# Moving the gate projections of a hybrid encoder layer beside its SSM, and two small transfers to another queue

## The chip, the cores and the metric

The kernel runs on one core of a Trainium2 chip. The metric is the time on the device of one execution, in microseconds (us), as the median of several runs. The engines are PE (TensorE), DVE (VectorE), ACT (ScalarE), POOL (GpSimd) and SP (SyncE, which here issues nearly all transfers).

## What is computed

One encoder layer in float32 on a sequence of 512 tokens of width 1024:

```python
h = h + 0.5 * swiglu_1(rms_norm(h))
u = rms_norm(h)
q, k, v, x_ssm, g_attn, g_ssm = split(u @ W_in)
y_attn = block_gqa(rope(qk_norm(q)), rope(qk_norm(k)), v) @ W_attn_branch
y_ssm  = glu(gelu(s5_fwd(x_ssm) + s5_bwd(x_ssm) + D * x_ssm)) @ W_ssm_branch
h = h + (sigmoid(g_attn) * y_attn + sigmoid(g_ssm) * y_ssm) @ W_out
h = h + 0.5 * swiglu_2(rms_norm(h))
h = h + sigmoid(rms_norm(h) @ W_ple_gate) * (p @ W_ple_proj)
```

There are 8 query heads of width 64 and 2 key/value heads. The SSM (a linear state-space scan in both directions) has 32 groups of 16 channels with 64 complex states each. g_attn and g_ssm are 1024 wide each, so with tiles of 128 channels there are 16 gate projections.

## The kernel before

Every float32 product is made of three matmuls: each operand is split into a high and a low part (`split`: a cast on ACT, then a subtraction on DVE), and `mm3` (lines 560 to 563) adds high x high, high x low and low x high. Weights come through `wchunk` (line 549): SP loads 512 KB into a raw tile (4 buffers), ACT writes the high part, DVE the low part. In names, w_399h and w_399l are the parts of such a weight.

The program order is: first FFN; input projections (V, K, Q, the SSM's input); the SSM's 16 blocks; the attention's 8 heads; the attention branch; W_out; second FFN; per-layer input. A Tile scheduler takes the instructions in this order, with priorities and its own estimate of engine times, and writes the order of each engine, so neighbouring steps are interleaved. On an engine the order is then fixed: an instruction that waits holds back all behind it on that engine or queue.

A gate projection is `gate(m)` (line 790): `proj_T` (line 763) loads one weight chunk, runs 24 matmuls of 128x512 (8 k-tiles, 3 each) against the input xh, xl (the tiles of `xg`) into a PSUM bank of tag "mm" (4 of these banks), then DVE multiplies by the norm's factor into ta[m] or ts[m] (line 794) and ACT applies a tanh (line 795). The table `NG1, NG2` (line 504) says how many of the 16 run where: the first NG1 ahead of the transposes of q and k (line 876), the next NG2 beside the SSM's blocks (loop at line 932), and the rest as fills beside the attention's heads.

In the SSM loop, `ssm_block(j)` (line 445) is issued at high priority: matmuls pv, DVE multiplications and two scans, a three-way split of the state (E, Er; `split3`, lines 30 to 36, which goes back and forth between ACT and DVE), matmuls py. `ssm_prefetch` (line 428) loads the next block's 1344 KB on SP (wv, tbl, wo, ml). At block 14 the scores of head 0 are issued too. Behind the loop, SP writes Z to zs_d in 8 pieces.

The attention goes head by head (lines 1051 to 1052): `run(values(hd), fill(hd), scores(hd + 1))` takes turns among three generators. `scores` (line 905): four score matmul pairs sc, a DVE row maximum nb (lines 918, 919), an exponential p on ACT with the row sum (line 921); at each odd head the reciprocals of the sums of two heads, and a write of these 1024 numbers to r_d, four bytes at a time (line 927). `values` (line 954): four times four transposes ppt of p (line 961), a split into ph and pl, two matmuls po (lines 966, 967); then the addition of two halves (ob on ACT, of on DVE, lines 972, 973); at each odd head R is read back from r_d, broadcast over partitions, in two pieces (line 977), `of` is multiplied by R (line 978) and split into oT, the input of the attention branch.

`fill(i)` (line 1023) is a head's third generator: with ng gates left, fills 0 to ng-1 are gates, the next two are halves of the GLU (each 24 matmuls; the first one calls `z_load`, line 985), the next four are halves of the SSM branch, later ones are empty. `z_load` issues four loads zT (line 993) of 256 KB from zs_d; each is split into z (ACT cast, DVE subtraction). The four zT take the slots of xl tiles 4 to 7, which the gates' matmuls read. Fills that remain after head 7 run in the loop at line 1053. Then come four halves of the attention branch, whose result is `attn_done` (line 1037): two multiplications, and a reload of h from h_d (line 1042; a gate ta[m] has lain in h's slot), 256 KB each, which W_out's epilogue (line 1059 on) needs.

Of the kernel before, what the change touches and what calls it, by code (L numbers as in the profile page):

```python
# [17 lines left out]
P = 128  # L18
# [406 lines left out]
NM = G // GM  # L425


def ssm_prefetch(nc, sp, k, j):

    d = k["ops"]  # L430
    b, q = j * GM // GB, j * GM % GB
    wv = sp.tile([P, 3, GM, 2 * P], BF16, tag="wv", name=f"wv{j}")
    nc.sync.dma_start(wv, d["wv"][b].rearrange("p (i g m) -> p i g m", i=3, g=GB)[:, :, q:q + GM])
    tb = sp.tile([P, 6, GM * NC_], F32, tag="tbl", bufs=2, name=f"tbl{j}")
    src = d["tb"][b].rearrange("p (i n) -> p i n", i=5)
    nc.sync.dma_start(tb[:, :5], src[:, :, q * NC_:(q + GM) * NC_])
    nc.sync.dma_start(tb[:, 5], src[:, 4, q * NC_:(q + GM) * NC_])
    wo = sp.tile([P, 3, GM, 2 * P], BF16, tag="wo", bufs=2, name=f"wol{j}")
    nc.sync.dma_start(wo, d["wo"][b].rearrange("p (i g m) -> p i g m", i=3, g=GB)[:, :, q:q + GM])
    mm = sp.tile([P, 3, GM, P], BF16, tag="m", bufs=2, name=f"ml{j}")  # L440
    nc.sync.dma_start(mm, d["m"][:, :, j * GM:(j + 1) * GM])
    return wv, tb, wo, mm
# [55 lines left out]
HD = 64  # L498
# [2 lines left out]
Q0, K0, V0, X0, GA0, GS0 = 0, 512, 640, 768, 1280, 2304  # L501
SSMW = 512

NG1, NG2 = 8, 4

SIDE = (5.5, 4.5, 3)

# [2 lines left out]
def kernel(  # L510
# [6 lines left out]
    nc = tc.nc  # L517
# [9 lines left out]
    def bank(tag, name):  # L527
        return ps.tile([P, 512], F32, tag=tag, bufs={"mm": 4, "pt": 2, "pv": 2}[tag], name=name)
# [3 lines left out]
    def uid(s):  # L532
        _u[0] += 1
        return f"{s}_{_u[0]}"
# [10 lines left out]
    def split(hi, lo, src):  # L545
        S.copy(hi, src)  # L546
        V.tensor_sub(lo, src, hi.bitcast(F32))  # L547
# [76 lines left out]
    h = [cp.tile([P, SEQ], F32, tag=f"h{m}", name=uid("h")) for m in range(KT)]  # L624
    h_d = dp.tile([KT, P, SEQ], F32, name="h_d")
# [134 lines left out]
    def slot(pool, tag, bufs, name, dt=F32):  # L760
        return pool.tile([P, SEQ], dt, tag=tag, bufs=bufs, name=uid(name))

    def proj_T(c0, done):

        wh, wl = wchunk(win[:, c0:c0 + P], KT, P)
        pg = bank("mm", uid("pi"))
        for k in range(KT):
            mm3(pg, wh[:, k], wl[:, k], xg[k][0], xg[k][1], k == 0, k == KT - 1)
            if k % 2 == 1 and k < KT - 1:
                yield  # L770
        done(pg)

    def run(*gens):

        gens = list(gens)
        while gens:
            gens = [g for g in gens if next(g, gens) is not gens]
# [12 lines left out]
    def gate(m):  # L790
        dst = (ta + ts)[m]

        def done(pg):
            V.tensor_mul(dst, pg, rb)
            S.activation(dst, dst, AF.Tanh, scale=0.5)

        return proj_T(GA0 + m * P, done)
# [107 lines left out]
    def scores(hd):  # L905

        g = hd // (NH // 2)
        pr = prs.setdefault(hd, [])
        nb = a0.tile([P, TT], F32, tag="nb", bufs=3, name=uid("nb"))
        if hd % 2 == 0:  # L910
            sums2[hd // 2] = a0.tile([P, 2, TT], F32, tag="s2", bufs=2, name=uid("s2"))
        sm = sums2[hd // 2][:, hd % 2]
        for t in range(TT):
            sc = bank("mm", uid("sc"))
            tk = slice(t * P, (t + 1) * P)
            T.matmul(sc, qT[hd][:, tk], kh[g], start=True, stop=False)
            T.matmul(sc, qT[hd][:, tk], kl[g], start=False, stop=True)  # L917
            V.tensor_reduce(nb[:, t:t + 1], sc, axis=AX.X, op=ALU.max, negate=True)  # L918
            V.tensor_mul(nb[:, t:t + 1], nb[:, t:t + 1], rq[:, t, hd:hd + 1])  # L919
            p_ = slot(pool_p[hd % 2], "pp", 4, "p")  # L920
            S.activation(p_, sc, AF.Exp, bias=nb[:, t:t + 1], scale=rq[:, t, hd:hd + 1], accum_out=sm[:, t:t + 1])  # L921
            pr.append(p_)
            yield
        if hd % 2 == 1:
            s2 = sums2[hd // 2]
            V.reciprocal(s2, s2)
            nc.sync.dma_start(r_d[hd // 2].rearrange("h (t p) -> p h t", p=P), s2)

    prs, sums2 = {}, {}
    r_d = [dp.tile([2, SEQ], F32, name=f"r_d{j}") for j in range(NH // 2)]  # L930
    Z = sp.tile([P, G, NC_], F32, tag="U", name="Z")
    for j in range(NM):
        with tc.high_priority():
            py = ssm_block(nc, sp, ps, pre, U3, j)
        if j < NM - 1:
            pre = ssm_prefetch(nc, sp, kd, j + 1)
        S.activation(Z[:, j * GM:(j + 1) * GM].rearrange("p g c -> p (g c)"), py[:, :GM * NC_], AF.Gelu_apprx_tanh)
        if j % 2 == 0 and j // 2 < NG2:
            run(gate(NG1 + j // 2))
        if j == NM - 2:  # L940
            run(scores(0))
    zv = zs_d.rearrange("(g c) (l n) -> l c g n", c=CH, l=L)
# [11 lines left out]
    def values(hd):  # L954
        pr = prs[hd]
        g = hd // (NH // 2)
        po = bank("pv", uid("po"))
        for kt in range(TT):
            pt = bank("pt", uid("ppt"))
            for t in range(TT):  # L960
                T.transpose(pt[:, t * P:(t + 1) * P], pr[t][:, kt * P:(kt + 1) * P], ident)  # L961
            ph, pl = ph_("ph", F32R), ph_("pl", F32R)
            split(ph, pl, pt)
            yield
            vv = vhl[:, kt, g].rearrange("p a d -> p (a d)")
            T.matmul(po, vv, ph, start=kt == 0, stop=False)
            T.matmul(po, vv, pl, start=False, stop=kt == TT - 1)
        if hd % 2 == 0:
            po_of[hd // 2] = slot(at, "of", 3, "of")
        of = po_of[hd // 2]  # L970
        ob = at.tile([HD, SEQ], F32, tag="ob", bufs=1, name=uid("ob"))
        S.copy(ob, po[HD:])
        V.tensor_add(of[(hd % 2) * HD:(hd % 2 + 1) * HD], po[:HD], ob)
        if hd % 2 == 1:
            R = at.tile([P, SEQ], F32, tag="R", bufs=1, name=uid("R"))
            for i in range(2):
                nc.sync.dma_start(R[i * HD:(i + 1) * HD], r_d[hd // 2][i].partition_broadcast(HD))
            V.tensor_mul(of, of, R)
            ohl.append(tuple(slot(at, f"o{c}{hd // 2}", 1, "oT", F32R) for c in "hl"))
            split(ohl[hd // 2][0], ohl[hd // 2][1], of)  # L980
# [56 lines left out]
    def attn_done(m, pg):  # L1037
        V.scalar_tensor_tensor(ta[m], ta[m], 1.0, pg, add, mul)
        mt = slot(at, "of", 3, "mt")
        V.scalar_tensor_tensor(mt, ts[m], 0.5, ta[m], mul, add)  # L1040
        h[m] = cp.tile([P, SEQ], F32, tag=f"h{m}", name=uid("h"))
        nc.sync.dma_start(h[m], h_d[m])
        if m < 4:
            mg.append((slot(mp, f"q{2 * m}", 1, "mg", F32R), slot(mp, f"q{2 * m + 1}", 1, "mg", F32R)))
        elif m < 6:
            mg.append((slot(mp, f"k{m - 4}h", 1, "mg", F32R), slot(mp, f"k{m - 4}l", 1, "mg", F32R)))
        else:
            mg.append((ph_("mg", F32R), ph_("mg", F32R)))
        split(mg[m][0], mg[m][1], mt)

    for hd in range(NH):
        run(values(hd), fill(hd), *([scores(hd + 1)] if hd < NH - 1 else []))
    for i in range(NH, 2 * KT - NG1 - NG2 + 6):
        run(fill(i))
    for mc in range(4):
        run(half(w["w_attn_branch"][0], mc, ohl, attn_done))
# [122 lines left out]
```

## Time and profile before

| | before |
|---|---|
| median of 3 runs | 1199.22 us (1196.43 to 1199.28) |
| profiled execution | 1200.59 us |
| span of its trace | 1198.8 us |
| granted TensorE clock, mean | 0.988 |
| PE busy | 1142.1 us (95%) |
| DVE busy | 772.8 us (64%) |
| ACT busy | 501.7 us (42%) |
| POOL busy | 48.3 us (4%) |

Times in the trace count from the start of the span. A granted clock of 1.0 is 2.4 GHz, 0.5 is 1.2 GHz. A wait or an idle time is shown with what ended it: "<-DVE pl L547" means that the engine went on when DVE's instruction of line 547 that writes pl was done. The mixing stage of this profile: input projections from 416 us, SSM from 466.4 to 592.5, attention to about 714, W_out from 728.4, second FFN from 776.

### The profile page before, as it was taken

The page shows a single profiled execution, that of the slowest core. Times are in us where ns is not written, and L with a number is a line of the kernel's source. Part 1 is how long each engine was busy: PE and PEld are TensorE (multiplying, and loading weights), DVE is VectorE, ACT ScalarE, POOL GpSimd, SP SyncE. Part 2 cuts the span into 40 slices and gives each one's busy share as a digit, 9 for nine tenths or more (in the row PEclk, how much of TensorE's full clock was granted, in tenths as well). Part 3 has the DMA queues.
Part 4 walks back from the last instruction along what each step waited for, and adds up shares of the span by engine and source line. Part 5 has one row for each costly group of instructions (what it writes and reads, how often), then busy time and mean ns, then how long its engine had stood idle before and what let it go on. Part 6 is the DMA issues. An engine that isn't in the chain of part 4 may idle for free.

```text
span 1198.8 us, 16348 instructions
## 1 busy us (share of the span) xinstructions
PE 1142.1 (95%) x6092; PEld 939.0 (78%) x6092; DVE 772.8 (64%) x1563; ACT 501.7 (42%) x914; POOL 48.3 (4%) x81
## 2 busy tenths in 40 slices
PE   4999979999999998988897999999999999999998
PEld 3788758888888887877786788888888888888886
DVE  3896799965899646998766857554543344544543
ACT  4583464542545424634465734332322232323331
POOL 4123100000000000000000000000000000000100
PEclk9999989999999999999998999999999999999999
DMA  9449754656967949797633125333223433223422
GB/s 185 136 103 309 240 204 154 202 141 155 299 210 238 299 132 138 213 265 221 181 89 62 51 74 171 109 88 101 82 73 98 138 91 104 79 73 97 151 61 53
DMA packets 258496, 175.97 MB, mean 147 GB/s; under 512 B 38928, under 2 KB 239824, under 8 KB 258416
## 3 DMA queue, kind: packets, MB, share of 16 engines
q1 hardware_dynamic: 254032, 162.66, 47.5%
q0 software_dynamic: 3920, 11.15, 3.6%
q10 hardware_dynamic: 464, 1.11, 0.5%
q8 instruction: 48, 0.79, 0.3%
q14 instruction: 32, 0.26, 0.1%
HBM read 148.89 MB, written 37.58 MB: 156 GB/s over the span
## 4 chain that ended last, share of the span: by engine, by line
PE 68%; DVE 14%; DMA 9%; ACT 4%; issue 3%; SPq 3%; ACTq 0%; DVEq 0%
PE pd L562 6%; PE pd L563 6%; PE pd L561 6%; PE pg L562 6%; PE pg L563 6%; PE pg L561 6%; PE pu L563 5%; PE pu L561 5%; PE pu L562 5%; DMA d_tb<-tst 3%; DMA w<-in_ffn_w_up_dram 2%; PE pi L561 1%; PE pi L562 1%; PE pi L563 1%; SPq L403 1%
## 5 line engine op out<-in xcount | busy, mean ns | idle before, releaser
L688 DVE TENSOR_TENSOR t<-pu,rb 128x512 f32<-128x512 f32 x44 | 30.3, 688 | 77.5 <-PE pu L563 77.3
L686 DVE TENSOR_TENSOR t<-pg,rb 128x512 f32<-128x512 f32 x44 | 30.3, 688 | 52.8 <-PE pg L563 50.9
L546 ACT CAST ah<-t 128x512 fp32r<-128x512 f32 x44 | 27.4, 622 | 55.1 <-DVE t L689 54.9
L706 DVE SCALAR_TENSOR_TENSOR h<-pd,h 128x512 f32<-128x512 f32 x32 | 22.0, 688 | 33.5 <-PE pd L563 33.4
L687 ACT ACTIVATE t<-t 128x512 f32<-128x512 f32 x44 | 27.7, 631 | 24.3 <-DVE t L686 23.7
L547 DVE TENSOR_TENSOR al<-t,ah 128x512 fp32r<-128x512 f32 x44 | 30.2, 686 | 6.5 <-ACT ah L546 6.2
L918 DVE TENSOR_REDUCE nb<-sc 128x1 f32<-128x512 f32 x32 | 21.6, 684 | 18.9 <-PE sc L917 18.8
L689 DVE TENSOR_TENSOR t<-t,t 128x512 f32<-128x512 f32 x44 | 30.3, 688 | 2.5 <-ACT t L687 0.4
L921 ACT ACTIVATE p<-sc,nb,rq 128x512 f32<-128x512 f32 x32 | 24.8, 780 | 9.7 <-DVE nb L919 9.7
L571 ACT ACTIVATE xh<-h,gains 128x512 fp32r<-128x512 f32 x32 | 22.7, 721 | 10.7 <-DVE h L706 7.7
L1084 POOL DMA_DIRECT2D pin<-in_p_dram x8 | 4.1, 525 | 550.3 <-PE pd L562 545.2
L547 DVE TENSOR_TENSOR pl<-ppt,ph 128x512 fp32r<-128x512 f32 x32 | 21.9, 684 | 6.6 <-ACT ph L546 6.6
L546 ACT CAST ph<-ppt 128x512 fp32r<-128x512 f32 x32 | 18.7, 588 | 14.3 <-PE ppt L961 14.2
L572 DVE SCALAR_TENSOR_TENSOR xl<-h,gains,xh 128x512 fp32r<-128x512 f32 x32 | 23.8, 743 | 0.7 <-ACT xh L571 0.3
L43 PE MATMUL pv<-U,wv 128*128 128x64 bf16 x384 | 14.3, 195 | 9.4 <-DMA wv<-d_wv 5.7
L961 PE MATMUL ppt<-ident,p 128*128 128x128 f32 x128 | 20.8, 278 | 2.0 <-ACT p L921 2.0
L43 PEld LDWEIGHTS <-wv 128*128 128x128 bf16 x384 | 12.5, 99 | 12.3 <-DMA wv<-d_wv 6.2
L961 PEld LDWEIGHTS ppt<-ident,p 128*128 128x128 f32 x128 | 16.6, 143 | 6.7 <-ACT p L921 2.4
L648 PE MATMUL xT<-ident,xt 128*128 128x128 f32 x32 | 7.8, 423 | 14.7 <-DMA xt<-in_x_dram 14.7
L43 PE MATMUL py<-E,wol 128*128 128x64 bf16 x384 | 17.5, 193 | 3.2 <-DVE E L36 3.2
L33 ACT CAST E<-vv 128x256 bf16<-128x256 f32 x16 | 6.5, 404 | 29.3 <-DVE vv L479 29.1
L648 PEld LDWEIGHTS xT<-ident,xt 128*128 128x128 f32 x32 | 6.3, 223 | 15.8 <-issue 14.3
(1966 smaller groups left out, 3885.8 us busy)
## 6 DMA issues: line engine op xcount, KB each, us to landing
w<-in_ffn_w_gate_dram SPq DMA_DIRECT2D x44, 512.0 KB
w<-in_ffn_w_up_dram SPq DMA_DIRECT2D x44, 512.0 KB
w<-in_w_in_dram SPq DMA_DIRECT2D x26, 512.0 KB
w<-in_ffn_w_down_dram SPq DMA_DIRECT2D x32, 384.0 KB
w<-in_ffn_w_down_dram SPq DMA_DIRECT2D x32, 320.0 KB
d_wo<-wo SPq DMA_DIRECT2D x8, 768.0 KB
d_wv<-wv SPq DMA_DIRECT2D x8, 768.0 KB
wv<-d_wv SPq DMA_DIRECT2D x16, 384.0 KB
```

The source lines that it names most:

```text
L43: nc.tensor.matmul(o, a[i], b[j], start=start and n == 0, stop=stop and n == 5)
L546: S.copy(hi, src)
L547: V.tensor_sub(lo, src, hi.bitcast(F32))
L561: T.matmul(o, ah, bh, start=start, stop=False)
L562: T.matmul(o, ah, bl, start=False, stop=False)
L563: T.matmul(o, al, bh, start=False, stop=stop)
L686: V.tensor_mul(t1, gu[0], rb)
L687: S.activation(t1, t1, AF.Silu)
L688: V.tensor_mul(t2, gu[1], rb)
L689: V.tensor_mul(t1, t1, t2)
L921: S.activation(p_, sc, AF.Exp, bias=nb[:, t:t + 1], scale=rq[:, t, hd:hd + 1], accum_out=sm[:, t:t + 1])
L961: T.transpose(pt[:, t * P:(t + 1) * P], pr[t][:, kt * P:(kt + 1) * P], ident)
```

## The change

The table of gate projections becomes 4 ahead of the transposes, 12 beside the SSM (blocks 0 to 15 get none or one each, three in four blocks), none beside the attention. So the fills move: the GLU halves from heads 4 and 5 to heads 0 and 1, the SSM-branch halves from heads 6, 7 and the two places behind them to heads 2 to 5, and heads 6 and 7 have no fill. And three kinds of transfer are issued by GpSimd's queue instead of SyncE's: the write of reciprocals to r_d, the two reads into R, and the reloads of h.

```diff
--- before.py
+++ after.py
@@ -501,7 +501,7 @@
 Q0, K0, V0, X0, GA0, GS0 = 0, 512, 640, 768, 1280, 2304
 SSMW = 512
 
-NG1, NG2 = 8, 4
+NG1, NG2 = 4, 12
 
 SIDE = (5.5, 4.5, 3)
 
@@ -924,7 +924,7 @@
         if hd % 2 == 1:
             s2 = sums2[hd // 2]
             V.reciprocal(s2, s2)
-            nc.sync.dma_start(r_d[hd // 2].rearrange("h (t p) -> p h t", p=P), s2)
+            nc.gpsimd.dma_start(r_d[hd // 2].rearrange("h (t p) -> p h t", p=P), s2)
 
     prs, sums2 = {}, {}
     r_d = [dp.tile([2, SEQ], F32, name=f"r_d{j}") for j in range(NH // 2)]
@@ -935,8 +935,8 @@
         if j < NM - 1:
             pre = ssm_prefetch(nc, sp, kd, j + 1)
         S.activation(Z[:, j * GM:(j + 1) * GM].rearrange("p g c -> p (g c)"), py[:, :GM * NC_], AF.Gelu_apprx_tanh)
-        if j % 2 == 0 and j // 2 < NG2:
-            run(gate(NG1 + j // 2))
+        for m in range(j * NG2 // NM, (j + 1) * NG2 // NM):
+            run(gate(NG1 + m))
         if j == NM - 2:
             run(scores(0))
     zv = zs_d.rearrange("(g c) (l n) -> l c g n", c=CH, l=L)
@@ -974,7 +974,7 @@
         if hd % 2 == 1:
             R = at.tile([P, SEQ], F32, tag="R", bufs=1, name=uid("R"))
             for i in range(2):
-                nc.sync.dma_start(R[i * HD:(i + 1) * HD], r_d[hd // 2][i].partition_broadcast(HD))
+                nc.gpsimd.dma_start(R[i * HD:(i + 1) * HD], r_d[hd // 2][i].partition_broadcast(HD))
             V.tensor_mul(of, of, R)
             ohl.append(tuple(slot(at, f"o{c}{hd // 2}", 1, "oT", F32R) for c in "hl"))
             split(ohl[hd // 2][0], ohl[hd // 2][1], of)
@@ -1039,7 +1039,7 @@
         mt = slot(at, "of", 3, "mt")
         V.scalar_tensor_tensor(mt, ts[m], 0.5, ta[m], mul, add)
         h[m] = cp.tile([P, SEQ], F32, tag=f"h{m}", name=uid("h"))
-        nc.sync.dma_start(h[m], h_d[m])
+        nc.gpsimd.dma_start(h[m], h_d[m])
         if m < 4:
             mg.append((slot(mp, f"q{2 * m}", 1, "mg", F32R), slot(mp, f"q{2 * m + 1}", 1, "mg", F32R)))
         elif m < 6:
```

What the scheduler makes of it is seen at three places. The first is SP's queue at the start of the attention (w_ are weight loads, zT the loads of z, r_d the write of reciprocals, R its reads). Before:

```order
L556 DMA w_7707<-in_w_ssm_branch_dram 128x4x256
L556 DMA w_7741<-in_w_attn_branch_dram 128x4x256
L993 DMA zT_7187<-zs_d 128x512
L993 DMA zT_7193<-zs_d 128x512
L993 DMA zT_7199<-zs_d 128x512
L927 DMA r_d_5031<-s_428_6857 128x8x1
L993 DMA zT_7205<-zs_d 128x512
L977 DMA R_7176<-r_d_5031 64x512 x2
L556 DMA w_7791<-in_w_attn_branch_dram 128x4x256
L556 DMA w_7841<-in_w_attn_branch_dram 128x4x256
L927 DMA r_d_5032<-s_483_7089 128x8x1
```

With the change:

```order
L944 DMA zs_d<-Z 16x32x64 x8
L556 DMA w_7381<-in_w_ssm_branch_dram 128x4x256
L556 DMA w_7495<-in_w_ssm_branch_dram 128x4x256
L556 DMA w_7741<-in_w_attn_branch_dram 128x4x256
L993 DMA zT_6855<-zs_d 128x512
L993 DMA zT_6861<-zs_d 128x512
L993 DMA zT_6867<-zs_d 128x512
L993 DMA zT_6873<-zs_d 128x512
L556 DMA w_7791<-in_w_attn_branch_dram 128x4x256
L556 DMA w_7841<-in_w_attn_branch_dram 128x4x256
L556 DMA w_7891<-in_w_attn_branch_dram 128x4x256
```

The four zT stand together, right behind the writes of Z and three weights; r_d and R are no longer in this queue.

The second is PE where the attention begins (py is the SSM's output, sc scores, ppt transposes, pi a gate, pg a GLU half). Before, from the last py:

```order
L43 MATMUL py_6670<-E_0_6662,wol_6587 128x64
L916 MATMUL sc_6615<-kh_4108,qT_4100 128x512
L917 MATMUL sc_6615<-kl_4110,qT_4100 128x512
L961 MATMUL ppt_6721<-ident,p_6599 128x128
L561 MATMUL pi_6736<-xh_297,w_399h 128x512
L562 MATMUL pi_6736<-xl_298,w_399h 128x512
L563 MATMUL pi_6736<-xh_297,w_399l 128x512
```

With the change, the scores of head 0 and the first matmuls behind them:

```order
L916 MATMUL sc_6707<-kh_4108,qT_4100 128x512
L917 MATMUL sc_6707<-kl_4110,qT_4100 128x512
L916 MATMUL sc_6714<-kh_4108,qT_4100 128x512
L917 MATMUL sc_6714<-kl_4110,qT_4100 128x512
L561 MATMUL pi_6813<-xh_297,w_401h 128x512
L562 MATMUL pi_6813<-xl_298,w_401h 128x512
L563 MATMUL pi_6813<-xh_297,w_401l 128x512
```

and what follows that gate's 24 matmuls and five of eight transposes:

```order
L961 MATMUL ppt_6912<-ident,p_6705 128x128
L961 MATMUL ppt_6912<-ident,p_6712 128x128
L961 MATMUL ppt_6912<-ident,p_6719 128x128
L561 MATMUL pg_6895<-z_6857,w_419h 128x512
L916 MATMUL sc_6903<-kh_4108,qT_4101 128x512
L917 MATMUL sc_6903<-kl_4110,qT_4101 128x512
L916 MATMUL sc_6934<-kh_4108,qT_4101 128x512
L917 MATMUL sc_6934<-kl_4110,qT_4101 128x512
L561 MATMUL pg_6952<-z_6857,w_419h 128x512
```

The scores of head 0 are followed by a whole gate projection, then by the transposes of two groups, then by the first GLU half and the scores of head 1. The gates w_399 to w_480 no longer stand between the heads; three whole or part gates (w_385, w_387, w_389) stand ahead of these scores.

The third is PE at the end of head 7 (po is the value product of the head, pg here the attention branch). Before, at the last po:

```order
L563 MATMUL pg_7747<-oT_7465,w_639l 128x512
L561 MATMUL pg_7769<-oT_6948,w_639h 128x512
L562 MATMUL pg_7769<-oT_6949,w_639h 128x512
L967 MATMUL po_7583<-pl_7650,vhl 128x512
L563 MATMUL pg_7769<-oT_6948,w_639l 128x512
L561 MATMUL pg_7769<-oT_7180,w_639h 128x512
L562 MATMUL pg_7769<-oT_7181,w_639h 128x512
L563 MATMUL pg_7769<-oT_7180,w_639l 128x512
```

and so on to the first matmul that needs the last oT:

```order
L561 MATMUL pg_7819<-oT_7465,w_650h 128x512
L562 MATMUL pg_7819<-oT_7466,w_650h 128x512
L563 MATMUL pg_7819<-oT_7465,w_650l 128x512
L561 MATMUL pg_7747<-oT_7669,w_639h 128x512
L561 MATMUL pg_7769<-oT_7669,w_639h 128x512
```

With the change:

```order
L961 MATMUL ppt_7719<-ident,p_7675 128x128
L966 MATMUL po_7685<-ph_7713,vhl 128x512
L967 MATMUL po_7685<-pl_7714,vhl 128x512
L966 MATMUL po_7685<-ph_7724,vhl 128x512
L967 MATMUL po_7685<-pl_7725,vhl 128x512
L561 MATMUL pg_7747<-oT_7737,w_639h 128x512
L561 MATMUL pg_7769<-oT_7737,w_639h 128x512
```

Between the last po and the first matmul on the last oT (of tile 3) there were 25 matmuls of the attention branch; now there is none, as these stand earlier.

## Rows read from the trace of the kernel before

**Rows 1.** The page: busy time by engine, and two of the costliest groups.
```profile
PE 1142.1 (95%) x6092; PEld 939.0 (78%) x6092; DVE 772.8 (64%) x1563; ACT 501.7 (42%) x914; POOL 48.3 (4%) x81
...
L918 DVE TENSOR_REDUCE nb<-sc 128x1 f32<-128x512 f32 x32 | 21.6, 684 | 18.9 <-PE sc L917 18.8
...
L921 ACT ACTIVATE p<-sc,nb,rq 128x512 f32<-128x512 f32 x32 | 24.8, 780 | 9.7 <-DVE nb L919 9.7
```

**Rows 2.** Windows: stretch, its length, busy us by engine, granted clock, DMA share, GB/s.
```profile
466.40:592.50 126.10, 114.63 (x1319) 95.33 (x1316) 116.25 (x274) 57.15 (x158) 0.76 (x1) 0.99 0.74 220
596.30:599.20 2.90, 2.90 (x9) 2.28 (x8) 0.00 (x0) 0.50 (x2) 0.00 (x0) 0.50 0.83 133
644.40:650.50 6.10, 6.10 (x17) 4.85 (x18) 1.72 (x5) 3.54 (x9) 0.00 (x0) 0.50 0.29 91
650.50:728.40 77.90, 77.38 (x371) 62.63 (x370) 58.53 (x97) 41.09 (x73) 0.00 (x0) 1.00 0.26 75
```

**Rows 3.** Waits of VectorE, 466.4 to 592.5: total us, times, longest.
```profile
DVE Er L34 <- ACT E L33: 3.9, 7, 0.8
```

**Rows 4.** TensorE's timeline at the start of the attention: start, length.
```profile
594.58 0.33 PE L961 MATMUL ppt<-ident,p 128*128 128x128 f32 x1 [2.00 <-ACT p L921]
...
597.84 0.63 PE L561 MATMUL pi<-xh,w_399h 128*128 128x512 f32 x1
598.26 0.63 PE L562 MATMUL pi<-xl,w_399h 128*128 128x512 f32 x1
```

**Rows 5.** TensorE's timeline, 636 to 645; idle before, and its releaser.
```profile
636.94 0.50 PE L967 MATMUL po<-pl,vhl 128*128 128x512 f32 x1 [1.06 <-DVE pl L547]
...
641.66 0.79 PE L967 MATMUL po<-pl,vhl 128*128 128x512 f32 x1 [3.55 <-DVE pl L547]
644.35 0.79 PE L966 MATMUL po<-ph,vhl 128*128 128x512 f32 x1 [1.90 <-ACT ph L546]
```

**Rows 6.** ScalarE's timeline, 632 to 643.
```profile
632.30 0.62 ACT L546 CAST z<-zT 128x512 fp32r<-128x512 f32 x1 [1.63 <-PE ppt L961]
632.95 0.58 ACT L972 COPY ob<-po 64x512 f32<-64x512 f32 x1
...
642.68 0.62 ACT L546 CAST z<-zT 128x512 fp32r<-128x512 f32 x1 [5.53 <-DMA zT<-zs_d]
```

**Rows 7.** The chain that ended last, 600 to 660: start, length, what.
```profile
599.82 0.24 PE pi L563
...
606.48 0.44 PE ppt L961 x4
...
632.53 10.13 DMA zT<-zs_d
```

**Rows 8.** SyncE's timeline of issues, 629 to 642.
```profile
629.58 1.68 SPq L993 DMA_DIRECT2D zT<-zs_d  x3
631.31 0.42 SPq L927 DMA_DIRECT2D r_d<-s  x1
632.53 0.32 SPq L993 DMA_DIRECT2D zT<-zs_d  x1
641.26 1.09 SPq L977 DMA_DIRECT2D R<-r_d  x2
```

**Rows 9.** GpSimd's transfers: count, KB each, median us from issue to landing.
```profile
gains<-in_mix_norm_dram POOLq DMA_DIRECT2D x1, 4.0 KB, 10.4
gains<-in_ple_norm_dram POOLq DMA_DIRECT2D x1, 4.0 KB, 7.6
...
trig<-in_consts_dram POOLq DMA_DIRECT2D x1, 256.0 KB, 4.0
```

**Rows 10.** VectorE's timeline, 706 to 712.
```profile
706.54 1.22 DVE L547 TENSOR_TENSOR w_672l<-w,w_672h 128x1024 fp32r<-128x1024 f32 x1 [0.16 <-ACT w_672h L546]
709.55 0.68 DVE L973 TENSOR_TENSOR of<-po,ob 64x512 f32<-64x512 f32 x1 [1.79 <-ACT ob L972]
710.27 0.69 DVE L978 TENSOR_TENSOR of<-of,R 128x512 f32<-128x512 f32 x1
711.65 0.69 DVE L547 TENSOR_TENSOR oT<-of,oT 128x512 fp32r<-128x512 f32 x1 [0.69 <-ACT oT L546]
```

## Prediction

> **What bounds the kernel now.** I read the page's busy times first, then the windows of the mixing stage, then the waits inside them. TensorE is busy for 1142.1 of the span's 1198.8 us [rows 1]: matmuls set the time wherever they have something to do, and the change alters no matmul, only when the sixteen gate projections run. So what matters is where TensorE stands idle between the SSM and the attention branch, and where VectorE bounds a stage.
>
> Three places show. First, the SSM stretch of 126.1 us: VectorE is busy for 116.25 of it, TensorE for 114.63 [rows 2]. the longest entry of VectorE's wait table there is 3.9 us in 7 pieces, short round trips to ScalarE for the three-way splits [rows 3]. VectorE is the bound. Second, the start of the attention: TensorE's timeline shows 2.00 us idle at 594.58 for the first softmax, after which matmuls start 0.42 us apart [rows 4] instead of the 0.23 that one takes in the chain of waits [rows 7]; the granted clock from 596.3 to 599.2 is 0.50 [rows 2], the lower of the two levels (1.2 and 2.4 GHz). Of those 2.90 us half is lost, 1.45. The place loses 2.00 + 1.45, about 3.5 us. Third, the z stall: TensorE waits 1.06, 3.55 and 1.90 us [rows 5], sum 6.51, and the 6.10 us behind it have clock 0.50 [rows 2], of which about 2.9 is lost. Together 9.4 us. Its cause stands in ScalarE's and SyncE's timelines: ScalarE is in order, and its fourth cast of z sits 5.53 us waiting for zT [rows 6]; the chain of waits has that load as its longest piece, 10.13 us [rows 7]. SyncE had issued three of the four loads at 629.58 (1.68 us), then the reciprocals' write at 631.31, and the fourth load at 632.53 [rows 8]. Nothing else that the trace shows lies ahead of the fourth but the 1024 four-byte pieces of that write, for which SyncE then waits until 641.26 to issue R. After 651 TensorE waits for nothing until the attention branch: 77.38 busy of 77.90 [rows 2].
>
> **The change part by part.** Durations are those of the profiled execution, 1200.59 us with a span of 1198.8; it lies 1.4 us above the median of the runs, 1199.22.
>
> *The z stall goes.* In the changed order z's four loads are issued at the start of the attention, ahead of any write of reciprocals, with no such write between them. They wait for the last gate's matmuls, which read the xl tiles whose slots they take. A load took 2.7 us from 629.58 to the first cast in ScalarE at 632.30 [rows 6, 8]; cast and subtraction add some 1.3. Between the first slot's release and the first GLU matmul the order has 10 gate matmuls and 8 transposes, 2.3 + 0.9 = 3.2 us, so about 0.9 us stays open: -9.4 + 0.9 = **-8.5**. Ends: -9.4 (all hidden) and -5 (half of the stall and its clock return, since SyncE first has three weight loads and eight writes of Z).
>
> Is it GpSimd that brings this? The row shows a load late behind small pieces; which engine issued them would not matter then. The Trainium skill, "DMA: Bandwidth & Descriptors", section "Issuing engines are not separate DMA queues", says that transfers from all issuing engines share the same 16 DMA engines and only issue time is saved; by it the other queue alone would give nothing here, and the gain would belong to the order of loads. No row of before separates the two.
>
> *Start of the attention, +0.8.* The first pair of heads' scores now come behind three gates, and one gate behind them, which must wait for a bank that scores of head 0 hold. From the start of those scores VectorE has a gate's multiplication, three reductions and a weight's subtraction [rows 1, 10], 0.69 + 3 x 0.68 + 1.22 = 3.95, and ScalarE one exponential of 0.78 [rows 1]: 4.7 us, 4.5 as instructions overlap a little, against 8 score matmuls of 0.23, 1.83. TensorE stands 2.7 and then loses about 1.6 at the low clock, 4.3 against 3.5 now. Ends: -3.5 (the scheduler's order hides it) and +3.
>
> *The heads become denser, +1.5.* Heads 0 to 5 have one 24-matmul fill each, as before, but GLU and SSM-branch halves in place of gates. In the changed order VectorE has 68.8 us of work there against 83 of TensorE, so it is not the bound; in the window after 650.5 of before the same kind of fill ran with TensorE idle for 0.52 of 77.90 us, VectorE busy for 58.53 [rows 2]. Ends: 0 and +4.
>
> *R's round trip moves to GpSimd, +0.7.* On SyncE the second pair's write and the read behind it are issued 9.95 us apart, and two reads take 1.09 us to issue [rows 8]; the multiplication with R starts 0.72 us behind the addition ahead of it, without a wait [rows 10]. On GpSimd nothing else is queued behind: its order is hb, four times write and two reads of R, then the eight reloads of h. The nearest rows are GpSimd's loads of 1024 four-byte pieces, 7.6 to 10.4 us from issue to landing, and its 256 KB load, 4.0 [rows 9]. Write plus two issues plus the second read is 7.6 + 1.1 + 4.0 = 12.7 to 10.4 + 1.1 + 4.0 = 15.5 us. From reciprocal to R multiplication VectorE's order holds 13.2, 13.3 and 14.2 us of own work for the first three pairs, and for the last 7.9, though there TensorE's order between them (29 + 17 matmuls at 0.23 and 7 groups of transposes at 0.44 [rows 7]) has 13.7 us, and some 2 us of chain follow. So it just fits; I take +0.7 for one pair being late by a little. Ends: 0, and +20 if each of four is late by 5.
>
> *The tail of heads 6 and 7, +5.7.* Before, 25 matmuls of the attention branch lay between the last value matmul and the first that needs oT of the last pair, and TensorE never waited. In the changed order nothing lies between: fills are used up and the scheduler has put those matmuls ahead. The chain of before is in VectorE's rows: L973 at 709.55, the multiplication with R at 710.27, the subtraction of oT at 711.65 [rows 10], so 2.1 us from the addition to the end of the cast between; ahead of it lie a cast and a copy by ScalarE, 0.6 each [rows 6], and a subtraction of 0.69 [rows 10], 1.9. With four value matmuls beside it: 2.1 + 1.9 + 0.2 - 0.9, 3.3 idle, 0.6 more between the last transposes, and half-clock matmuls behind it for 1.8, as at the two places above. Ends: 3 and 7.
>
> *TensorE's own work between,* -0.7 (119.2 against 118.5 us between the last py and w_out's first matmul, counted over both orders with the pitches above).
>
> *SSM stretch, +1.6.* Though 12 gates are now issued beside the SSM and 4 ahead of it, both orders hold 11 gate multiplications and 256 VectorE rows between the last U and the last E: the scheduler had already spread the 8. What differs is by how much ScalarE's round trips are exposed between VectorE's rows: 10.0 us against 8.4, counted over both orders. The queue has one more weight load of 512 KB (16 against 15) beside DMA engines that are 0.74 busy [rows 2]. Ends: -3 and +4. The reloads of h on GpSimd cost nothing: they are issues on a queue with nothing else behind, and a load of this size took GpSimd 4.0 us [rows 9], where the first w_out epilogue is more than ten away; if that cover is gone, an epilogue is late by a microsecond.
>
> Sum: -8.5 + 0.8 + 1.5 + 0.7 + 5.7 - 0.7 + 1.6 = **+1.1**, so 1201.7 for such an execution and 1200.3 against the median.
>
> **The rivals.** *R is late (slower), 0.2.* R's multiplication stands in VectorE's order ahead of work for TensorE. As soon as write, wake-up and reads take more than some 16 us, VectorE stops four times a pass; at 20 us each stop is 4, with the clock following it: 4 x 4 = 16, in place of the 0.7 already counted: 1215.6. For it: the fit has little to spare at its upper end, and GpSimd's small-piece loads scatter from 7.6 to 10.4 [rows 9]; against it: those were loads in the traffic of the start, and the heads load little.
>
> The Trainium skill, "SBUF — State Buffer", section "🔬 SBUF: two separate sides", warns that transfers from GpSimd stall when VectorE holds a shared port in a two-port copy; by it such a price would come only where copies run. The work of VectorE between reciprocal and R is tensor-tensor and reduction, no copy, and no row of before has GpSimd issue beside it, so the rule gets little weight.
>
> *Tail and heads are covered (faster), 0.28.* If the order hides the end of head 7 as heads hid their ends before (TensorE waits only where VectorE is behind), tail and density fall to 1 us in sum: 1.1 - 6.2 is -5.1, 1194. For it: the window after 650.5 has no stall of that kind. Against: the order has nothing between.
>
> *The SSM stretch moves, 0.12.* VectorE bounds it. If weight loads push an SSM load back by a few us, the term is +4 and the time 1202.7; if ScalarE's round trips fall under other work, -3 and 1195.7.
>
> *The change does little of what it says, 0.1.* Loads of z could be as late as now, since SyncE still waits for slots: then -8.5 shrinks to -3 and the time is 1205.8.
>
> **How the numbers follow.** The forecast has 0.3 by itself. 0.3% of 1199 is 3.6 us, about what a measurement tells from no change. Faster: the covered tail (0.25 of its 0.28) and the lower end of forecast and SSM (0.07), 0.32. Slower: late R (0.2), late z (0.08), the upper end of forecast and SSM (0.06), 0.34. Same: what is left, 0.34. Range 1191 to 1211: below, the ends 0 for heads, 3 for the tail and -3 for the SSM; above, two or three late reads, or the upper ends of tail, heads and SSM with half of a late z. The forecast's own range is 1196 to 1206.
>
> **What would show it.** z's four loads in one group and no ScalarE wait for zT over 1.5 us; TensorE idle about 2.7 us before the gate that follows the first scores; 3 to 4 us idle ahead of the first attention-branch matmul of the last pair, clock 0.5 behind it; VectorE's wait for R under 1 us. A VectorE wait on R of several us in each pair, or no idle at the tail, would make the forecast wrong.

## The result, and the profile after

The changed kernel takes 1207.46 us (median of 7 runs, 1202.68 to 1209.42) against 1199.28 (7 runs, 1196.43 to 1203.1): a ratio of 1.006, 95% interval 1.0041 to 1.0079, slower by about 0.6%. Its profiled execution took 1209.14 us with a span of 1207.4; its mean granted clock is 0.982 against 0.988.

Where the 8.6 us of span went, worked out from the starts of four instructions (first pv, end of the last py, first matmul of W_out, end):

| stretch | before | after | difference |
|---|---|---|---|
| start to first pv | 465.9 | 467.4 | +1.5 |
| SSM: first pv to last py | 126.2 | 136.0 | +9.8 |
| attention and its branch | 136.4 | 133.1 | -3.3 |
| W_out to end | 470.4 | 470.9 | +0.5 |

The first row is scatter: the order of work up to there is nearly the same in all kernels of this study, and their first pv stands between 463.2 and 468.2. So the attention and its branch gained 3.3 us, and the SSM stretch lost three times as much. Windows of the changed kernel (columns as in [rows 2]), first the whole stretch, then pieces of it:

```profile
467.40:603.37 135.97, 119.79 (x1332) 100.69 (x1332) 116.84 (x273) 57.23 (x158) 0.76 (x1) 0.94 0.69 204
506.50:526.50 20.00, 12.37 (x183) 10.60 (x181) 19.45 (x58) 9.97 (x19) 0.76 (x1) 0.91 0.82 240
526.50:546.50 20.00, 19.19 (x202) 16.77 (x203) 17.31 (x41) 5.36 (x12) 0.00 (x0) 0.84 0.59 177
546.50:566.50 20.00, 15.33 (x209) 12.90 (x206) 17.04 (x43) 6.18 (x14) 0.00 (x0) 1.00 0.85 250
566.50:585.00 18.50, 18.50 (x217) 15.54 (x213) 13.30 (x30) 6.12 (x12) 0.00 (x0) 0.91 0.77 225
```

Against [rows 2] VectorE has the same work (116.84 us against 116.25), but TensorE is busy 119.79 us for the same matmuls (1332 records; from first pv to last py of before it was 114.71 for 1329), because the granted clock was 0.94 instead of 0.99, and it is idle for 16.2 us instead of 11.5. So of the 9.8 us some 5 are the lower clock and some 5 are idle. In the piece from 506.5 TensorE works for 12.37 of 20 us. TensorE's waits in the stretch, changed kernel (total us, times, longest):

```profile
PE py L43 <- DMA ml<-d_m: 7.5, 4, 3.5
PE pv L43 <- DMA wv<-d_wv: 6.0, 2, 4.4
PE pv L43 <- DVE U L36: 3.7, 1, 3.7
PE py L43 <- DVE E L36: 2.6, 3, 1.2
```

and before:

```profile
PE pv L43 <- DMA wv<-d_wv: 5.7, 4, 2.0
...
PE py L43 <- DMA ml<-d_m: 1.7, 2, 1.3
```

The loads of the SSM are waited for 13.5 us instead of 7.4. Where, TensorE's timeline shows. Changed kernel, 514 to 528:

```profile
514.72 0.39 PE L563 MATMUL pi<-xh,w_353l 128*128 128x512 f32 x1
514.95 1.36 PE L882 MATMUL qt<-ident,qs 128*128 128x128 f32 x11
516.14 0.86 PE L43 MATMUL pv<-U,wv 128*128 128x64 bf16 x24
...
518.60 0.74 PE L882 MATMUL qt<-ident,qs 128*128 128x128 f32 x5
523.73 1.46 PE L43 MATMUL pv<-U,wv 128*128 128x64 bf16 x24 [4.38 <-DMA wv<-d_wv]
527.31 0.50 PE L43 MATMUL py<-U,ml 128*128 128x64 bf16 x6 [2.12 <-DMA ml<-d_m]
```

and before, 518 to 524:

```profile
519.40 0.39 PE L563 MATMUL pi<-xh,w_355l 128*128 128x512 f32 x1
...
521.21 0.39 PE L562 MATMUL pi<-xl,w_357h 128*128 128x512 f32 x1
521.44 0.41 PE L43 MATMUL py<-E,wol 128*128 128x64 bf16 x8
523.68 0.87 PE L43 MATMUL pv<-U,wv 128*128 128x64 bf16 x24 [1.83 <-DMA wv<-d_wv]
```

The wv of that block lands at the same time in both, 523.7. Before, gates w_355 and w_357 and a few matmuls py fill TensorE until 521.85 and it waits 1.83. In the changed kernel the fourth and last gate ahead of the transposes ends at 514.95; what follows are the transposes qt, the SSM blocks and kt, and no gate until 532.6. TensorE stands for 4.38 and 2.12 us, and the clock falls (0.91 and 0.84 in the windows above). The gates not run there are run at the end of the stretch, between the last blocks, where pv and py now wait behind them in TensorE's order: the round trips of [rows 3] are 4.4 us instead of 3.9, but VectorE also waits 3.0 us for pv and 2.3 for a gate.

```profile
DVE Er L34 <- ACT E L33: 4.4, 8, 0.8
DVE tt L463 <- PE pv L43: 3.0, 2, 1.8
DVE ts L794 <- PE pi L563: 2.3, 1, 2.3
```

Not every stall is a lack of gates. From 562.8 TensorE waits 3.47 us for an ml (ending at 566.29), and matmuls of gates w_375 and w_377 stand behind that block's py in the order and wait with it. SyncE had issued that load only at 561.12:

```profile
561.12 0.61 SPq L441 DMA_DIRECT2D ml<-d_m  x1
```

In the attention part the terms of the forecast are found again. The four loads of z are issued together, and ScalarE no longer waits for one; the low clock stands at the start of the attention and at the tail. SyncE and TensorE, changed kernel:

```profile
628.82 2.39 SPq L993 DMA_DIRECT2D zT<-zs_d  x4
```

```profile
PE pi L561 <- ACT p L921: 2.9, 1, 2.9
PE pg L561 <- ACT oT L546: 2.8, 1, 2.8
PE po L967 <- DVE pl L547: 0.7, 3, 0.2
PE pg L561 <- ACT z L546: 0.3, 1, 0.3
```

These answer [rows 5] and [rows 8]: 0.3 us for z instead of 6.51. GpSimd's transfers, count, KB each and median us to landing:

```profile
R<-r_d POOLq DMA_DIRECT2D x8, 128.0 KB, 3.4
r_d<-s POOLq DMA_DIRECT2D x4, 4.0 KB, 10.6
```

The write lands after 10.6 us, the read after 3.4: with two issues of 1.04 together, 15.0 from reciprocal to R, at the upper end of the bounds from [rows 9], and VectorE's wait table for this kernel's heads has no entry for R.

### The profile page after: what moved, and what is told of

Its sections match the earlier page's. It is cut to its first block, busy times and chain, and to the rows that moved or that the text cites. A ratio compares the mean times of both kernels' runs of the same rounds, so it can differ in the third digit from the quotient of the medians.

```text
span 1207.4 us, 16341 instructions
## 1 busy us (share of the span) xinstructions
PE 1148.2 (95%) x6092; PEld 944.4 (78%) x6092; DVE 772.3 (64%) x1563; ACT 502.9 (42%) x914; POOL 60.9 (5%) x101
## 4 chain that ended last, share of the span: by engine, by line
PE 70%; DVE 12%; DMA 9%; ACT 3%; SPq 3%; issue 3%; ACTq 0%; DVEq 0%
PE pd L562 6%; PE pd L563 6%; PE pd L561 6%; PE pg L562 6%; PE pg L561 6%; PE pg L563 6%; PE pu L561 5%; PE pu L563 5%; PE pu L562 5%; DMA d_tb<-tst 2%; DMA w<-in_ffn_w_up_dram 2%; PE pi L561 2%; PE pi L562 2%; PE pi L563 2%; SPq L403 1%
## 5 line engine op out<-in xcount | busy, mean ns | idle before, releaser
L43 PEld LDWEIGHTS <-wv 128*128 128x128 bf16 x384 | 13.4, 102 | 13.5 <-DMA wv<-d_wv 7.0
L794 DVE TENSOR_TENSOR ts<-pi,rb 128x512 f32<-128x512 f32 x8 | 5.5, 691 | 22.2 <-PE pi L563 22.0
```

The source lines that it names most:

```text
L43: nc.tensor.matmul(o, a[i], b[j], start=start and n == 0, stop=stop and n == 5)
```

## The experiments

Three theories stood at first. The cover theory: with only four gates ahead of the transposes TensorE has nothing to run while SSM loads land late. Its rivals: the transfers on GpSimd cost the time (queue theory), or sixteen weight loads ahead of the attention are too many for the DMA engines (load theory).

**Only the queues.** The three transfer lines of the change, with gates 8/4/4 and the old loop.

> Gates 8/4/4 as before, only the three kinds of transfer on GpSimd. Cover theory (the 8 us are lost in the SSM stretch, because with 4 gates ahead TensorE has no gate matmuls to run while SSM loads are late): SSM stretch (first pv to last py) 126 us as before. If small pieces in one queue delay the fourth zT, its landing falls from 10.1 us to about 3 and the time to 1191 to 1194; if the engine of issue does not matter, the z stall stays at 6 to 7 us of idle and the time is 1199. Queue theory (GpSimd's reads of R or reloads of h cost the 8 us): 1205 to 1208.

Measured: 1201.3 us, ratio 1.0002 (0.9988 to 1.0016), stretch 125.6. The queue theory falls for this order of work. And the z stall is all there, although no write of reciprocals stands in SyncE's queue any more. SyncE, ScalarE and GpSimd in this run:

```profile
631.12 3.28 SPq L993 DMA_DIRECT2D zT<-zs_d  x4
```

```profile
645.08 0.62 ACT L546 CAST z<-zT 128x512 fp32r<-128x512 f32 x1 [6.09 <-DMA zT<-zs_d]
```

```profile
632.74 0.92 POOL L927 DMA_DIRECT2D r_d<-s  x1 [10.72 <-DVE s L926]
```

The write leaves GpSimd at 632.74, ahead of the fourth load, and ScalarE gets that load only at 645.08. The chain of waits has it as one piece:

```profile
634.08 10.98 DMA zT<-zs_d
```

So the load is as late with the 1024 small pieces in the other queue (10.98 us against 10.13 in [rows 7]). The Trainium skill says in "DMA: Bandwidth & Descriptors", section "Issuing engines are not separate DMA queues", that transfers run on the same 16 DMA engines and interleave there, whichever engine started them; the measurement agrees with it. The gain of the change at this place comes from the order of the loads: in the next run, with all transfers on SyncE and the new order, TensorE waits 0.3 us for z.

**Only the gates.** The table and the loop of the change, all transfers left on SyncE:

```diff
-NG1, NG2 = 8, 4
+NG1, NG2 = 4, 12
...
-        if j % 2 == 0 and j // 2 < NG2:
-            run(gate(NG1 + j // 2))
+        for m in range(j * NG2 // NM, (j + 1) * NG2 // NM):
+            run(gate(NG1 + m))
```

> Gates 4/12/0, all transfers on SyncE. Cover theory: SSM stretch 134 to 137 us as in the changed kernel, time 1206 to 1208; TensorE's order is the same as in the changed kernel. Queue theory: 1198 to 1200. Should R on SyncE delay weight loads of the heads, it shows as TensorE waits on weights in the heads.

Measured: 1204.05 us, ratio 1.003 (1.0018 to 1.0043), stretch 131.3. Slower, as the cover theory has it, but by half of the change's loss and with less than the 134 to 137 us expected for the stretch. The changed kernel was then run again:

> The changed kernel once more, beside the runs that follow, to see how far its time scatters: 1204 to 1208, SSM stretch 131 to 137 us. If GpSimd's transfers are what sets it 0.3% above the same gates with transfers on SyncE, it stays at 1207; if that gap is scatter, it comes to 1204 to 1205.

Measured: 1207.05 us, ratio 1.0065 (1.0048 to 1.0082), stretch 134.7: the gap of 0.3% is no scatter of one batch. TensorE, VectorE and ScalarE have the same order in the changed kernel's trace and in the run with only the gates, and in the SSM stretch SyncE and GpSimd too. Both have the first idle place (3.63 and 2.30 us in the run with only the gates). They part at one wait for ml. Only gates:

```profile
565.02 0.44 PE L43 MATMUL py<-U,ml 128*128 128x64 bf16 x9 [2.03 <-DMA ml<-d_m]
```

```profile
567.20:583.00 15.80, 15.80 (x204) 13.30 (x203) 13.32 (x30) 6.34 (x12) 0.00 (x0) 1.00 0.91 266
```

Changed kernel, with the clock of 0.91 behind it, from 566.5 to 585, that stands in the windows above (2.62 us and 0.91 in the repeated run):

```profile
566.29 0.44 PE L43 MATMUL py<-U,ml 128*128 128x64 bf16 x9 [3.47 <-DMA ml<-d_m]
```

Behind 2.03 us of idle the clock stayed at 1.00, behind 2.62 and 3.47 it fell. The length of a stall alone does not decide this: the runs with 8/8/0 and 4/8/4, reported below, have 2.60 us of idle at 524.84 and 2.98 at 599.35 with a clock of 1.00 behind it, and before it was 0.50 behind 2.00 us [rows 2, 4]. First 8/8/0, then 4/8/4:

```profile
524.84 0.87 PE L43 MATMUL pv<-U,wv 128*128 128x64 bf16 x24 [2.60 <-DMA wv<-d_wv]
```

```profile
524.84:534.84 10.00, 10.00 (x141) 8.67 (x142) 9.59 (x22) 3.56 (x8) 0.00 (x0) 1.00 0.87 250
```

```profile
599.35 0.50 PE L561 MATMUL pi<-xh,w_393h 128*128 128x512 f32 x1 [2.98 <-ACT p L921]
```

```profile
599.35:605.14 5.79, 5.79 (x26) 4.77 (x27) 0.62 (x5) 2.78 (x8) 0.00 (x0) 1.00 0.25 84
```

The longer wait with the slower matmuls behind it, 1.4 us and about 1.7 (0.09 of 18.5 us), accounts for most of the 4.7 us between the stretches (3.4 for the repeated run). Why ml lands later when transfers of a later stage sit in another queue stays open; no run was made for it.

**Eight ahead, none beside the attention.** The run that separates the load theory from the cover theory:

```diff
-NG1, NG2 = 4, 12
+NG1, NG2 = 8, 8
```

> Gates 8/8/0, transfers on GpSimd: 8 gates stay ahead of the transposes and none beside the attention. Cover theory: SSM stretch back to 126 to 128, attention part (last py to first matmul of W_out) 133 as in the changed kernel, time 1195 to 1198. Load theory (16 weight loads beside or ahead of the SSM are too many for the DMA engines): stretch 133 or more, time 1205 to 1208.

Measured: 1197.57 us, ratio 0.9981 (0.9965 to 0.9998); stretch 128.3, attention part 131.9. As many weight loads are made ahead of the attention as in the changed kernel, and the loss is gone: the load theory falls. Two further executions of these gates, with the transfers on GpSimd again and on SyncE:

> Gates 8/8/0 on GpSimd once more, on the same chip as the two others: 1196 to 1199, ratio to before 0.996 to 1.000.

> Gates 8/8/0 with all transfers on SyncE. If the engine of issue does not matter, 1196 to 1199, the same as 8/8/0 on GpSimd. If the 0.3% between the changed kernel and the same gates on SyncE is a cost of GpSimd's issues, it is faster than 8/8/0 on GpSimd by 3 us.

Measured: 1197.46 us, ratio 0.9983 (0.997 to 0.9997), and 1197.63 us, ratio 0.9985 (0.9971 to 0.9998). Stretches 126.8 and 126.9. The engine of issue makes no difference here. 8/8/0 beats the kernel before by 0.2%, in three runs whose intervals end just below 1, and the changed kernel by 0.8%. TensorE's load waits in the last of them:

```profile
PE pv L43 <- DMA wv<-d_wv: 7.1, 4, 2.6
...
PE py L43 <- DMA ml<-d_m: 0.8, 2, 0.6
```

**Four ahead, four beside the attention.** `NG1, NG2 = 4, 8`.

> Gates 4/8/4, transfers on GpSimd: 4 ahead as in the changed kernel, but as many gates beside the attention as before. Cover theory: SSM stretch 133 to 137, and the attention part as in before or a little better, time 1207 to 1211. Load theory: fewer loads beside the SSM, stretch 127 to 129, time 1199 to 1201.

Measured: 1216.84 us, ratio 1.0132 (1.0115 to 1.0149), stretch 139.2. Fewer loads beside the SSM and the slowest of all: the four gates ahead decide, not the count beside. Some 3 us of this stretch are not the SSM's: the last blocks stand behind head 0's scores here, and the wait of 2.98 us for its softmax lies in front of the last py. The attention part was 140.3, since here the z stall came back beside the other costs, a wait of 9.2 us in one piece. SyncE's four loads and GpSimd's write of reciprocals fell together again:

```profile
643.59 2.62 SPq L993 DMA_DIRECT2D zT<-zs_d  x4
```

```profile
644.27 0.92 POOL L927 DMA_DIRECT2D r_d<-s  x1 [9.32 <-DVE s L926]
```

This run also answers a rival. The GLU brings a small load on GpSimd, hb (512 numbers, four bytes at a time); in the changed kernel it is issued at 519.90, beside the first stall, and before only at 584.1. Here it comes at 592.81, and the first stall is there all the same:

```profile
521.98 0.88 PE L43 MATMUL pv<-U,wv 128*128 128x64 bf16 x24 [3.96 <-DMA wv<-d_wv]
525.46 0.50 PE L43 MATMUL py<-U,ml 128*128 128x64 bf16 x6 [2.59 <-DMA ml<-d_m]
```

**Six ahead.** `NG1, NG2 = 6, 10`.

> Gates 6/10/0, transfers on GpSimd. Cover theory: between the two, as two gates more than in the changed kernel stand ahead of the transposes: stretch 129 to 133, time 1199 to 1204. If a threshold and not the cover decides, it equals 8/8/0 (128 us, 1197.6) or 4/12/0 (136 us, 1207).

Measured: 1201.21 us, ratio 1.0018 (1.0003 to 1.0033), stretch 130.4. It lies between, as cover by gates would have it: with none beside the attention the stretch is 126.8 to 128.3 us for eight ahead, 130.4 for six and 131.3 to 136.0 for four.

**Without most loads of ml.** In both kernels the matrices ml were loaded for block 0 and used in all:

```diff
-    mm = sp.tile([P, 3, GM, P], BF16, tag="m", bufs=2, name=f"ml{j}")
-    nc.sync.dma_start(mm, d["m"][:, :, j * GM:(j + 1) * GM])
-    return wv, tb, wo, mm
+    if j == 0:
+        k["mm0"] = sp.tile([P, 3, GM, P], BF16, tag="m", bufs=2, name=f"ml{j}")
+        nc.sync.dma_start(k["mm0"], d["m"][:, :, j * GM:(j + 1) * GM])
+    return wv, tb, wo, k["mm0"]
```

> The changed kernel, but the matrices ml (192 KB for each SSM block) are loaded for the first block alone and used in all; the output is not the reference's. Late-load theory (TensorE idles where loads of the SSM land late and no gate stands ahead in its order): the waits for ml (7.5 us) go and the stretch falls from 136 to 125 to 129, time 1196 to 1200. Order theory (VectorE is kept waiting by gates that stand ahead of pv in TensorE's order, loads or not): the stretch stays above 132.

> The kernel before with the same loads left out, as a control (output not the reference's). Late-load theory: only 1.7 us of waits for ml to win, stretch 124 to 126, time 1196 to 1199. Order theory: the same.

Measured: 1205.59 us, ratio 1.0048 (1.003 to 1.0065), and 1207.81 us, ratio 1.0069 (1.0047 to 1.0091). The stretches were as expected, 127.3 and 124.6, the times were not. In the first, TensorE now waits for wv instead, and the clock is 0.78 behind it:

```profile
PE pv L43 <- DMA wv<-d_wv: 8.7, 4, 3.9
...
PE py L43 <- DMA wol<-d_wo: 2.4, 1, 2.4
```

```profile
523.00:543.00 20.00, 18.39 (x190) 16.14 (x189) 15.44 (x36) 5.07 (x11) 0.00 (x0) 0.78 0.48 136
```

The attention part grew to 139.7; by the last py 28 fewer matmul records than in the changed kernel had passed, some 6 us of work at 0.23 each. In the second it grew to 147.3 with a larger z stall (7.0 us in its longest wait). With the loads gone the scheduler had written another order for TensorE, VectorE, ScalarE and SyncE, so the pair does not measure the price of ml alone. How much of the loss is late loads, and how much the gates that stand ahead of pv and py at the end, was therefore not separated. What the pair shows is that a shorter stretch is worth nothing where its gates are only put off.

**Scores beside the last gate.** On 8/8/0, an attempt at the start of the attention:

```diff
         for m in range(j * NG2 // NM, (j + 1) * NG2 // NM):
-            run(gate(NG1 + m))
-        if j == NM - 2:
-            run(scores(0))
+            run(gate(NG1 + m), *([scores(0)] if j == NM - 1 else []))
```

> Gates 8/8/0 on GpSimd as in the run g8_8, but the scores of head 0 take turns with the last gate instead of standing ahead of it, so that their softmax runs beside the gate's matmuls. If the 2.9 us of idle at the start of the attention come from the gate that waits for a score's bank, idle there falls below 1.7 us, the low clock behind it goes, and the time is 3 to 4 us under that of 8/8/0: 1193 to 1195. If the wait moves on to the transposes of the first head, 1196 to 1198.

Measured: 1199.88 us, ratio 1.0 (0.9983 to 1.0016): above both ranges expected, and 2.3 to 2.4 us above the two last runs of 8/8/0, though the intervals of the ratios overlap. The idle of 2.9 us is gone, and others took its place: 1.6 us for z, 3.5 in seven pieces for pl, and 4.9 instead of 2.8 at the tail, where VectorE waits for R:

```profile
DVE of L976 <- DMA R<-r_d: 7.9, 4, 4.0
```

```profile
708.06 0.68 DVE L971 TENSOR_TENSOR of<-po,ob 64x512 f32<-64x512 f32 x1 [1.21 <-ACT ob L970]
710.96 0.69 DVE L976 TENSOR_TENSOR of<-of,R 128x512 f32<-128x512 f32 x1 [2.21 <-DMA R<-r_d]
```

With denser heads the round trip, here 15.0 to 16.7 us from reciprocal to multiplication, no longer fits: R is late in all four pairs.

## Why the prediction came out as it did

The time lies inside the wide range and on the side that had the largest chance together with no change (slower, 0.34), but the point was 7 us too low, and the time lies outside the forecast's own range of 1196 to 1206. What stood behind the upper end of the wide range, late reads of R, or the upper ends of tail, heads and SSM with a late z, did not come, but for the SSM's, whose end of +4 was passed. That the range holds the time is luck. The signs named came nearly all (the idle ahead of the last pair was 2.77 instead of 3 to 4), and none of them looked at the SSM stretch. By its steps:

*The z stall goes: right.* -8.5 was forecast, 6.51 us of idle and 2.9 of low clock became 0.3 us, -9.1. That the order of the loads brings it and not the other queue, which the text left open, is shown by the run with only the queues.

*Start of the attention: right in mechanism, too small.* +0.8 was forecast. The idle was 2.87 us (2.7 forecast); the low clock behind it lasted from 622.45 to 628.58, with matmuls 0.43 us apart, so it cost 2.9 instead of 1.6. In sum 5.7 against 3.5, +2.2.

*Denser heads, R: nothing.* Between start and tail TensorE waits 0.8 us in four short pieces, the 0.3 us for z among them, and VectorE never for R; +1.5 and +0.7 became about 0.

*The tail: right, a little smaller.* +5.7 was forecast; 2.77 us idle, 0.45 between the last transposes, and about 1.3 lost to the clock until 724.05 are 4.5. These terms sum to -9.1 + 2.2 + 4.5 = -2.4; with the -0.7 of the forecast for TensorE's own work that is -3.1, and measured were -3.3.

*The SSM stretch: this step failed.* The text counted VectorE's rows (256 in both orders), called VectorE the bound, and took +1.6 with ends -3 and +4; measured were +9.8, and +8.5 in the repeated run. VectorE's work was indeed the same. But the count of gates in the stretch says nothing about where they stand in it. VectorE, which was to bound the stretch, was idle for 19.1 us of it instead of 9.9. In the piece where TensorE stands it is nearly full (19.45 of 20.00 us); its idle time comes at the end. Before, then after:

```profile
565.00:592.03 27.03, 25.31 (x303) 21.02 (x302) 24.51 (x55) 10.93 (x22) 0.76 (x1) 1.00 0.70 218
```

```profile
567.00:603.37 36.37, 34.72 (x376) 28.77 (x373) 25.70 (x52) 12.61 (x23) 0.00 (x0) 0.95 0.61 184
```

It idles 10.7 us there instead of 2.5. Before, gates w_355 to w_361 stood beside the middle blocks, just where wv and ml of those blocks land late; the change took four gates from there and put them behind the transposes. TensorE's idle time is not free there, because the two engines are nearly balanced (114.63 and 116.25 us in [rows 2]): time that TensorE loses in the middle comes back as gates ahead of pv and py at the end. And some stalls are paid twice, through the clock: of 9.8 us, 5 are matmuls at a lower clock, a cost for which the term had no place. The DMA share of 0.74 in [rows 2] was read as a risk for loads to come later; at the first stall wv in fact came at the same microsecond, and it was the work in front of it that was missing. The ml of the stall at 562.8 was indeed late, as the rival had it: issued 1.7 us before TensorE came to it, it landed after 5.1.

*The rivals.* Late R did not come in the changed kernel, but it did when the heads became denser (four waits, 7.9 us), so its place was rightly described, and about rightly its limit (round trips of 15.0 to 16.7 us there, some 16 in the text); the price there was 7.9 us of VectorE's time in all. The covered tail did not come. The rival on the SSM stretch named late loads as the cause, with +4 where +9.8 was measured.

*VectorE and GpSimd's transfers.* The rule of the Trainium skill ("SBUF — State Buffer", section "🔬 SBUF: two separate sides") that transfers issued by GpSimd stall beside VectorE's two-port copies got little weight in the text, and no such stall shows beside tensor-tensor and reduction work: from a write of reciprocals to the read behind it GpSimd took 10.2 to 12.0 us in the changed kernel, and SyncE 9.95 in [rows 8] and 9.2 to 11.6 in the run with only the gates.

## What to carry to other kernels

Before filler work is moved, list what each piece covers where it stands now, by the waits of the engine that runs it: filler beside late loads is worth its time, and the same filler put later did not make up for it here. Equal counts of instructions in a stretch are no evidence of equal time; read the order inside it. Count a stall on TensorE together with the low clock behind it, which here often, but not always, cost about as much as the stall. And test the two parts of a double change apart: the queues alone did nothing here, and half of the move of the gates (8/8/0) is a gain of 0.2%.

## What the runs showed of the hardware

Where the write of 1024 four-byte pieces was under way, on SyncE's queue or on GpSimd's, a 256 KB load was late by some 8 us: 10.98 us in the chain of waits of the run with only the queues, against 2.7 for the first such load in [rows 6, 8]. And the same TensorE order had a granted clock of 1.00 behind an idle time of 2.03 us and 0.91 behind 2.62 or 3.47 at the same place, which together with the longer wait is most of the difference between the stretches of these runs; at other places it stayed at 1.00 behind 2.60 and 2.98 us and fell to 0.50 behind 2.00.
